# A fill order that also asks for free PSUM banks: the two attentions of an encoder trunk on one Trainium2 core

## The chip, the core and the metric

The kernel runs on one NeuronCore of a Trainium2 chip. The metric is the device time of one launch in microseconds (us), median of several runs. The engines have one instruction queue each, in order: TensorE (PE in the profile), VectorE (DVE), ScalarE (ACT), GpSimd (POOL) and SyncE (SP), which issues nearly all DMAs.

## The reference, cut to what matters

512 tokens of width 1024 go through two layers, all in fp32. Layer A is differential attention with rotary positions, layer B chunked attention with a relative bias over keys and values that are projected once; each is followed by a SwiGLU FFN, and a LayerNorm closes every part.

```python
# layer A, for each of 8 heads and each block i of 128 queries (kend = 128 * (i + 1))
sc = einsum('bqhmd,bkhmd->bhmqk', q[:, q0:kend], k[:, :kend])      # m: two maps
p = softmax(where(allowed, sc, neg)); a = p[:, :, 0] - lam * p[:, :, 1]
outs.append(einsum('bhqk,bkhe->bqhe', a, v[:, :kend]))
...
o = rms_norm(concatenate(outs), subln_g) * (1.0 - lambda_init)     # then @ w_o
# layer B, for each of 16 heads
p = softmax(q @ k_band + bias); o = p @ v_band                     # then @ w_o
# behind each: x = layer_norm(alpha * x + mix); x = layer_norm(alpha * x + swiglu(x))
```

## The kernel before

Every fp32 operand of a large product is split into a high and a low part that TensorE takes at its fast rate, so a projection step is three matmuls (high by high, high by low, low by high) of 512 or 256 columns. All instructions of all engines are written in the order in which the Python program runs; nothing reorders them later. That order comes from a model in the program: `Modelled` and `Model` keep, for each block of a tile, when it is written (`there`) and when it is last used (`used`), by fixed costs per engine, and `clk[0]` is the modelled time of TensorE. `later` and `chain` put the work of the other engines into a list with a modelled time; it is issued when `clk[0]` has come that far.

**Attention A** (lines 1053 to 1136, `unit_a` and `attention_a`) has 32 units, 8 heads by 4 query blocks. A unit has four steps on TensorE: `s`, the scores `sc`, in one bank for each of the two maps; `at`, the transposes of the mixed probabilities `e`; `o`, the product with the values; `ot`, the transpose of the normalised result `sq`. Between `s` and `at` stands the chain for `e`: on DVE a masked pass over each bank of scores with a row maximum (`CUSTOM_DVE_ANT_0`), on ACT two exponentials, on DVE a reciprocal, a factor `c` and the mix. Between `at` and `o` ACT copies `aT`; between `o` and `ot` ACT squares, POOL takes a power and DVE scales (`sq`). `STEPS` says which unit each step takes in an iteration: s(i), o(i-2), ot(i-3), at(i-1). **Attention B** (`unit_b`, `values_b`, `attention_b`) has 8 pairs of heads by 4 query blocks; its steps are `s` (`sc_b`), `at` (transposes `pt_b`) and, once for each pair, `v` (`po`).

Between these steps stand **fills**: matmuls of the projections of later heads (`q_ps`, `k_ps`, `va_ps`; in layer B `bq_ps`, `bk_ps`, `vb_ps`) and, when these are through, of the first part of the output projection (`oa`, `ob`). `weave` takes both streams. A number from the attention is a wish for so many ns of fill, kept as a credit. A function from it is a wait: fill is issued until the function says yes, and what was issued counts as credit, so that less follows. The waits of before ask by `there` whether what a step reads is written in the model.

PSUM has eight banks here: the pool `psp` holds two for each of the names `pj` (projections), `sm`, `sc0` and `sc1`. In attention A a unit's scores take both banks of `sc0`, `at` and `ot` take those of `sm` in turn, `o` those of `sc1`. In attention B the scores take `sc0`, and `pt_b` and `po` take one of `sm` and one of `sc1`. A matmul that opens a bank waits on the chip until the last reader of what stood there is through; in the model that only moves `clk[0]` (`model.unused` in `passed`).

Of the kernel before, what the change touches and what calls it, by code (L numbers as in the profile page):

```python
# [19 lines left out]
P = 128  # L20
# [8 lines left out]
HALF = 512  # L29
# [104 lines left out]
def trunk(ctx, tc, x, a_w_qkv, a_lambda, a_subln_g, a_w_o, kv_w, b_w_q, b_rel_bias, b_w_o,  # L134
          ln_g, ln_b, ffn_w_in, ffn_w_out, cos_t, sin_t, out):
    nc = tc.nc
    model = Model()
# [13 lines left out]
    psp = ctx.enter_context(tc.tile_pool(name="psp", bufs=2, space=PS))  # L151
# [3 lines left out]
    clk = [0.0]  # L155
    popped = [0.0]
    serial = itertools.count()
    pending = []
    slots = {}

    def name_of(a):
        return a.tensor.name
# [27 lines left out]
    def there(*tiles, late=0.0):  # L190

        names = [name_of(t) for t in tiles]
        return not any(n in p_[3] for p_ in pending for n in names) and all(
            model.ready(t) + late <= clk[0] for t in tiles)

    def mm(out_, lhsT, rhs, start, stop, cost=1.0):
        settle([name_of(lhsT), name_of(rhs)])
        nc.tensor.matmul(out_, lhsT, rhs, start=start, stop=stop)  # L198
        passed(out_, (lhsT, rhs), cost * (out_.free_size() / 2.4 + 13), start)
# [34 lines left out]
    def tick(everything=False):  # L234
        while pending and (everything or min(pending)[0] <= clk[0]):
            run_first()
# [580 lines left out]
    values_done = [0]  # L817
# [118 lines left out]
    qk = {}  # L936
# [88 lines left out]
    vt = []  # L1025
# [81 lines left out]
    def attention_a():  # L1107
        units = [(h, qt) for h in range(HA) for qt in range(NT)]
        live = {}
        nu = len(units)  # L1110
        for i in range(nu + max(step[1] for step in STEPS if step[0] != "fill")):
            rates = FA[0] if i < FA[2] else FA[1] if i < nu else FA[3]
            for kind, n in STEPS:
                if kind == "fill":
                    yield rates[n]
                    continue
                if not 0 <= i - n < nu:
                    continue
                h, qt = units[i - n]
                if kind == "s":  # L1120
                    yield lambda: h in qk
                    yield lambda: there(*qk[h])
                    live[i] = [unit_a(h, qt), None]
                    done["n"] = i + 1
                elif kind == "o":
                    yield lambda: 2 * values_done[0] > h and there(live[i - n][1], vt[0][:, h * P:(h + 1) * P])
                else:
                    yield lambda: there(live[i - n][1])
                if kind == "at":
                    done["s"] = i - n == nu - 1  # L1130
                live[i - n][1] = next(live[i - n][0])
                if kind == "ot":
                    del live[i - n]
                    done["o"] = h - (qt < NT - 1)
        tick(True)
# [31 lines left out]
    x1d = [dram.tile([S, D], F32, name=f"x1d_{l}") for l in range(2)]  # L1167

    weave(attention_a(), fill(FILL_A, qk_a, "va", o_proj(oTh, oTl, lambda t: x[0, t * P:(t + 1) * P, :], 0, "oa")))
    tick(True)  # L1170
    phase.close()
# [59 lines left out]
    qk = {}  # L1231
# [7 lines left out]
    vt = []  # L1239
# [12 lines left out]
    held = {}  # L1252
# [33 lines left out]
    biases = {}  # L1286
# [66 lines left out]
    def attention_b():  # L1353
        units = [(p, qt) for p in range(HB // 2) for qt in range(NT)]
        live = {}
        nu = len(units)
        load_bias(0)
        for i in range(nu + max(step[1] for step in STEPS_B if step[0] != "fill")):
            rates = FB[0] if i < FB[2] else FB[1] if i < nu else FB[3]
            for kind, n in STEPS_B:  # L1360
                if kind == "fill":
                    yield rates[n]
                    continue
                if not 0 <= i - n < nu:
                    continue
                p, qt = units[i - n]
                if kind == "s":
                    yield lambda: p in qk
                    yield lambda: there(*qk[p], *biases[p])
                    live[i] = [unit_b(p, qt), None]  # L1370
                    live[i][1] = next(live[i][0])
                    done["n"] = i + 1
                elif kind == "at":
                    yield lambda: there(live[i - n][1])
                    done["s"] = i - n == nu - 1
                    next(live.pop(i - n)[0])
                elif kind == "v" and qt == NT - 1:
                    yield lambda: there(*held[p][1], *held[p][2])
                    values_b(p)
                    done["o"] = p  # L1380
                    yield FBV
                elif kind == "prep":
                    if qt == 1:
                        prepare_b(p)
                    if qt == PREP_B:
                        yield lambda: 2 * values_done[0] > p
                        split_values(p)
                    if qt == NT - 1 and p + 1 < HB // 2:
                        load_bias(p + 1)
        tick(True)  # L1390
# [50 lines left out]
```

## Time and profile before

| | |
|---|---|
| median of 3 runs | 1220.28 us (1219.87 to 1220.51) |
| the profiled execution | 1220.33 us, its span 1218.6 us |
| PE busy | 1186.4 us (97% of the span) |
| DVE busy | 880.6 us (72%) |
| ACT, POOL busy | 554.7 us (46%), 428.2 us (35%) |
| mean granted TensorE clock | 0.994 of full speed |

The span runs from the first to the last instruction of the profiled execution; its time has 1.7 us more around that. Attention A with its fills lies from 47 us to about 223 us, the first FFN and what leads to layer B up to 610 us, attention B up to about 830 us, and the second FFN is the rest. PE rows at line 198 are `mm`, at line 203 transposes; most rows of the other engines are at line 76, where the model issues them, so they are told apart by their tiles. A PE row's length has the pipeline in it: the rate is read from the starts of rows that follow each other.

### The profile page before, as it was taken

The page shows a single profiled execution, that of the slowest core. Times are in us where ns is not written, and L with a number is a line of the kernel's source. Part 1 is how long each engine was busy: PE and PEld are TensorE (multiplying, and loading weights), DVE is VectorE, ACT ScalarE, POOL GpSimd, SP SyncE. Part 2 cuts the span into 40 slices and gives each one's busy share as a digit, 9 for nine tenths or more (in the row PEclk, how much of TensorE's full clock was granted, in tenths as well). Part 3 has the DMA queues.
Part 4 walks back from the last instruction along what each step waited for, and adds up shares of the span by engine and source line. Part 5 has one row for each costly group of instructions (what it writes and reads, how often), then busy time and mean ns, then how long its engine had stood idle before and what let it go on. Part 6 is the DMA issues. An engine that isn't in the chain of part 4 may idle for free.

```text
span 1218.6 us, 20002 instructions
## 1 busy us (share of the span) xinstructions
PE 1186.4 (97%) x7640; PEld 1076.5 (88%) x7640; DVE 880.6 (72%) x1451; ACT 554.7 (46%) x1049; POOL 428.2 (35%) x410
## 2 busy tenths in 40 slices
PE   7999999999999999999999999989999999999997
PEld 7878888789999999888897998968999999998886
DVE  3688797489999998431745677674899999983327
ACT  3467666344444444332236676662454444433220
POOL 1126253414666663001223242213236665510022
PEclk9999999999999999999999999999999999999999
DMA  8444232443555444423244243315433333352321
GB/s 262 127 105 121 75 102 85 162 139 103 149 146 148 143 122 150 136 96 128 97 131 132 75 122 95 105 52 190 122 104 104 105 104 105 105 196 98 104 70 69
DMA packets 164192, 145.75 MB, mean 120 GB/s; under 512 B 6096, under 2 KB 137456, under 8 KB 164096
## 3 DMA queue, kind: packets, MB, share of 16 engines
q1 hardware_dynamic: 164096, 144.47, 39.5%
q8 instruction: 60, 0.98, 0.3%
q14 instruction: 36, 0.29, 0.1%
HBM read 127.63 MB, written 13.67 MB: 116 GB/s over the span
## 4 chain that ended last, share of the span: by engine, by line
PE 90%; DVE 6%; ACT 2%; issue 1%; POOL 1%; DMA 0%; DVEq 0%; SPq 0%; ACTq 0%; POOLq 0%
PE m L198 31%; PE gu L198 6%; PE c L198 5%; PE a L198 5%; PE b L198 5%; PE d L198 4%; PE vb_ps L198 4%; PE bk_ps L198 3%; PE bq_ps L198 3%; PE va_ps L198 3%; PE k_ps L198 3%; PE q_ps L198 3%; PE ob L198 2%; PE oa L198 2%; PE sc_b L198 2%; PE po L198 1%
## 5 line engine op out<-in xcount | busy, mean ns | idle before, releaser
L76 POOL TENSOR_TENSOR sums<-raw_u 128x512 f32<-128x512 f32 x38 | 48.9, 1288 | 167.7 <-DVE s3lo L76 148.7
L76 POOL TENSOR_TENSOR lo_fo<-raw_fo,hi_fo 128x1024 fp32r<-128x1024 f32 x8 | 19.1, 2389 | 215.8 <-ACT hi_fo L76 215.8
L76 ACT ACTIVATE sg<-sg 128x512 f32<-128x512 f32 x38 | 24.0, 632 | 137.8 <-DVE sg L76 137.8
L76 POOL TENSOR_TENSOR sums<-raw_g,sums 128x512 f32<-128x512 f32 x38 | 75.4, 1984 | 0.0
L76 POOL TENSOR_TENSOR sums<-raw_g,raw_u 128x512 f32<-128x512 f32 x38 | 68.7, 1808 | 0.0
L76 DVE TENSOR_TENSOR alo<-raw_g,ahi 128x1024 fp32r<-128x1024 f32 x38 | 67.4, 1773 | 0.1
L76 ACT CAST s3hi<-sums 128x1024 fp32r<-128x1024 f32 x38 | 40.0, 1052 | 59.6 <-POOL sums L76 59.6
L76 ACT CAST hi_fk<-raw_fk 128x1024 fp32r<-128x1024 f32 x28 | 29.5, 1052 | 74.6 <-PE d L198 71.1
L76 DVE TENSOR_TENSOR lo_fk<-raw_fk,hi_fk 128x1024 fp32r<-128x1024 f32 x28 | 33.9, 1221 | 26.9 <-ACT hi_fk L76 26.9
L76 POOL TENSOR_TENSOR sums<-sums,raw_g 128x512 f32<-128x512 f32 x38 | 51.6, 1357 | 3.9 <-DMA raw_g<-in_ffn_w_in_dram 1.1
L76 DVE TENSOR_TENSOR s1lo<-sums,s1hi 128x1024 fp32r<-128x1024 f32 x38 | 48.3, 1271 | 0.0
L76 DVE TENSOR_TENSOR ulo<-raw_u,uhi 128x512 fp32r<-128x512 f32 x38 | 46.7, 1228 | 0.0
L76 ACT CAST hi_fo<-raw_fo 128x1024 fp32r<-128x1024 f32 x16 | 16.9, 1054 | 64.5 <-PE d L198 64.5
L76 DVE TENSOR_TENSOR s3lo<-sums,s3hi 128x1024 fp32r<-128x1024 f32 x38 | 46.1, 1214 | 0.1
L76 POOL TENSOR_TENSOR rs<-rs,mexp 128x1 f32<-128x1 f32 x16 | 15.8, 987 | 79.4 <-DVE rs L76 79.4
L76 DVE TENSOR_TENSOR m<-m,m 128x256 f32<-128x256 f32 x76 | 31.6, 416 | 15.9 <-PE m L198 15.9
L198 PE MATMUL m<-T1h,s1hi 128*128 128x256 f32 x152 | 43.0, 283 | 0.0
L198 PE MATMUL m<-T1l,s1hi 128*128 128x256 f32 x152 | 43.0, 283 | 0.0
L198 PE MATMUL m<-T1h,s1lo 128*128 128x256 f32 x152 | 43.0, 283 | 0.0
L198 PE MATMUL m<-T2g,s1hi 128*128 128x256 f32 x152 | 43.0, 283 | 0.0
L198 PE MATMUL m<-T2b,s1hi 128*128 128x256 f32 x152 | 43.0, 283 | 0.0
L198 PE MATMUL m<-T2g,s1lo 128*128 128x256 f32 x152 | 43.0, 283 | 0.0
(612 smaller groups left out, 4814.0 us busy)
## 6 DMA issues: line engine op xcount, KB each, us to landing
raw_g<-in_ffn_w_in_dram SPq DMA_DIRECT2D x44, 512.0 KB, 4.0
raw_u<-in_ffn_w_in_dram SPq DMA_DIRECT2D x44, 512.0 KB, 5.2
raw_fk<-in_ffn_w_out_dram SPq DMA_DIRECT2D x28, 512.0 KB, 3.7
raw_fo<-in_ffn_w_out_dram SPq DMA_DIRECT2D x16, 512.0 KB, 3.7
skew<-extd SPq DMA_DIRECT2D x16, 320.0 KB, 6.1
raw_va<-in_a_w_qkv_dram SPq DMA_DIRECT2D x8, 512.0 KB, 4.9
raw_q<-in_a_w_qkv_dram SPq DMA_DIRECT2D x8, 512.0 KB, 5.0
raw_k<-in_a_w_qkv_dram SPq DMA_DIRECT2D x8, 512.0 KB, 4.5
```

The costliest lines, as they stand in the source:

```text
L76: return issue(*args, **kwargs)
L198: nc.tensor.matmul(out_, lhsT, rhs, start=start, stop=stop)
```

## The change

A new function `clear` asks of the model whether the banks that the next step will open are out of use: of each name it takes as many of the oldest banks as the step needs, and wants that no deferred instruction names them and that their last modelled use is not after `clk[0]`. Every wait ahead of a step on TensorE in both attentions now asks for that too, so that fills are issued until then. No instruction is added or removed.

```diff
+    def clear(*tags):
+
+        names = [n for tag in dict.fromkeys(tags) for n in slots[(psp.name, tag)][-2:][:tags.count(tag)]]
+        return not any(n in p_[3] for p_ in pending for n in names) and all(
+            model.used.get((n, i), 0.0) <= clk[0] for n in names for i in range(HALF // P))
...
-                    yield lambda: there(*qk[h])
+                    yield lambda: there(*qk[h]) and clear("sc0", "sc0")
...
-                    yield lambda: 2 * values_done[0] > h and there(live[i - n][1], vt[0][:, h * P:(h + 1) * P])
+                    yield lambda: 2 * values_done[0] > h and there(live[i - n][1], vt[0][:, h * P:(h + 1) * P]) and clear("sc1")
                 else:
-                    yield lambda: there(live[i - n][1])
+                    yield lambda: there(live[i - n][1]) and clear("sm")
...
-                    yield lambda: there(*qk[p], *biases[p])
+                    yield lambda: there(*qk[p], *biases[p]) and clear("sc0", "sc0")
...
-                    yield lambda: there(live[i - n][1])
+                    yield lambda: there(live[i - n][1]) and clear("sm", "sc1")
...
-                    yield lambda: there(*held[p][1], *held[p][2])
+                    yield lambda: there(*held[p][1], *held[p][2]) and clear("sm", "sc1")
```

The order on TensorE differs in three stretches, which in the trace of before lie at 77.9 to 136.6 us and 164 to 223 us (attention A) and at 722 to 776 us (attention B); on the other engines instructions move by a few places inside the same stretches. In the changed kernel line 198 has become 204 and line 203 has become 209. In the rows below the first number behind a name is the query block of the unit (for `sc` and `pt_b` the map or head follows), and the last one only tells buffers apart.

**First stretch, TensorE, from the transposes of the first head's query block 3 (77.91 us in the trace) on.** Before:

```order
L203 MATMUL at_3_889<-ident,e_3_733 128x128 x4
L198 MATMUL sc_1_0_921<-ks_779,qs_715 128x256
...
L198 MATMUL o_3_931<-va_323,aT_3_897 128x128
...
L203 MATMUL ot_2_941<-ident,sq_2_883 128x128
L198 MATMUL q_ps_849<-xTh_a,hi_q_708 128x512
...
L203 MATMUL at_0_962<-ident,e_0_873 128x128
L198 MATMUL sc_2_0_973<-ks_779,qs_715 128x384
...
L198 MATMUL o_0_983<-va_323,aT_0_964 128x128
L198 MATMUL q_ps_849<-xTh_a,hi_q_708 128x512
...
L203 MATMUL ot_3_1016<-ident,sq_3_938 128x128
```

And with the change:

```order
L209 MATMUL at_3_889<-ident,e_3_733 128x128 x4
L204 MATMUL q_ps_849<-xTh_a,hi_q_708 128x512
...
L204 MATMUL sc_1_0_958<-ks_779,qs_715 128x256
...
L209 MATMUL ot_2_979<-ident,sq_2_883 128x128
L209 MATMUL at_0_986<-ident,e_0_873 128x128
L204 MATMUL k_ps_938<-xTh_a,hi_k_804 128x512
...
L204 MATMUL sc_2_0_1018<-ks_779,qs_715 128x384
...
L204 MATMUL o_0_1028<-va_323,aT_0_989 128x128
L209 MATMUL ot_3_1045<-ident,sq_3_976 128x128
L209 MATMUL at_1_1052<-ident,e_1_965 128x128 x2
L204 MATMUL sc_3_0_1065<-ks_779,qs_715 128x512
```

Between `at_3` and `sc_1` stand now 24 fills where there were none, between `ot_2` and `at_0` none where there were 9, and between `at_0` and `sc_2` 12 where there were none. From `sc_2` to `at_2` no fill is left; before, 21 fills stood between `at_0` and `at_2`.

**Second stretch, VectorE, the sixth head's query blocks 2 and 3 (184 us in the trace).** Before:

```order
L76 ISA e_3_2181,nm_3_2182<-sc_3_1_2176,mask 128x512
...
L76 TENSOR_TENSOR krc_2208<-kr_2201,cosb 128x512
L76 TENSOR_TENSOR lo_oa_0_2213<-raw_oa_0_1726,hi_oa_0_2211 128x1024
L76 TENSOR_TENSOR lo_oa_1_2216<-raw_oa_1_1846,hi_oa_1_2214 128x1024
L76 TENSOR_TENSOR oTl<-ot_0_2196,oTh 128x128
L76 RECIPROCAL r_3_2184<-s_3_2183 128x2
...
L76 SCALAR_TENSOR_TENSOR e_3_2181<-e_3_2181,c_3_2263 128x512
```

And with the change:

```order
L76 ISA e_2_2126,nm_2_2127<-sc_2_1_2121,mask 128x384
...
L76 TENSOR_TENSOR krc_2168<-kr_2161,cosb 128x512
L76 TENSOR_TENSOR lo_oa_0_2173<-raw_oa_0_1726,hi_oa_0_2171 128x1024
L76 TENSOR_TENSOR lo_oa_1_2176<-raw_oa_1_1846,hi_oa_1_2174 128x1024
...
L76 SCALAR_TENSOR_TENSOR e_2_2126<-e_2_2126,c_2_2248 128x384
L76 ISA e_3_2261,nm_3_2262<-sc_3_0_2251,mask 128x512
...
L76 SCALAR_TENSOR_TENSOR e_3_2261<-e_3_2261,c_3_2347 128x512
```

The two low parts `lo_oa` stood between the masked pass and the mix of query block 3; they now stand between those of query block 2. Between `sc_2` and `at_2` of that block 90 fills are written on PE.

**End of attention A, TensorE, from the last head's first scores (204.99 us in the trace).** Before:

```order
L203 MATMUL at_2_2547<-ident,e_2_2428 128x128 x3
L198 MATMUL sc_0_0_2552<-ks_2321,qs_2170 128x256
...
L198 MATMUL o_2_2570<-va_323,aT_2_2551 128x128
...
L203 MATMUL ot_1_2577<-ident,sq_1_2512 128x128
...
L203 MATMUL at_3_2592<-ident,e_3_2495 128x128 x4
L198 MATMUL sc_1_0_2598<-ks_2321,qs_2170 128x256
```

And with the change:

```order
L209 MATMUL at_2_2541<-ident,e_2_2465 128x128 x3
...
L204 MATMUL sc_0_0_2559<-ks_2254,qs_2255 128x256
...
L204 MATMUL o_2_2569<-va_323,aT_2_2546 128x128
...
L209 MATMUL ot_1_2578<-ident,sq_1_2529 128x128
L209 MATMUL at_3_2581<-ident,e_3_2517 128x128 x4
L204 MATMUL sc_1_0_2600<-ks_2254,qs_2255 128x256
```

Before, three fills stood behind `sc_0` and three behind `ot_1`, the last ahead of the units that run out without any. Now three stand ahead of `sc_0`, none follows, and all other fills have moved further forward. In attention B the moves are smaller: at 723 us, 24 fills of 256 columns that stood behind `sc_b_3` now stand as 36 ahead of `pt_b_1`, and later groups move by three to six matmuls.

## Rows read from the trace of the kernel before

**Rows 1.** The page's chain that ended last, by engine:

```profile
PE 90%; DVE 6%; ACT 2%; issue 1%; POOL 1%; DMA 0%; DVEq 0%; SPq 0%; ACTq 0%; POOLq 0%
```

**Rows 2.** Windows: us, busy by engine, granted PE clock, DMA share, GB/s:

```profile
76.60:136.60 60.00, 57.10 (x353) 49.70 (x353) 49.77 (x135) 41.22 (x121) 27.35 (x43) 1.00 0.39 105
...
164.00:209.00 45.00, 43.31 (x279) 38.22 (x277) 37.10 (x99) 29.25 (x86) 18.90 (x32) 1.00 0.33 95
209.00:223.00 14.00, 10.26 (x55) 8.36 (x56) 8.08 (x30) 7.50 (x28) 4.23 (x12) 0.88 0.01 3
...
722.00:776.00 54.00, 53.96 (x304) 46.61 (x303) 40.53 (x111) 37.45 (x98) 15.71 (x29) 1.00 0.33 98
```

**Rows 3.** PE's waits, whole span: waited for: us in total, times, longest:

```profile
PE pt_b L203 <- DVE e_b L76: 5.3, 3, 2.8
PE at L203 <- DVE e L76: 3.8, 3, 1.5
...
PE at L203 <- DVE oTl L76: 1.0, 1, 1.0
```

**Rows 4.** PE timeline, first stretch: start, length, line, operation [idle before, releaser]:

```profile
77.91 0.60 PE L203 MATMUL at<-ident,e 128*128 128x128 f32 x4
...
80.26 0.48 PE L198 MATMUL q_ps<-xTh_a,hi_q 128*128 128x512 f32 x1
...
84.06 0.30 PE L203 MATMUL at<-ident,e 128*128 128x128 f32 x1 [1.45 <-DVE e L76]
...
92.02 0.49 PE L203 MATMUL at<-ident,e 128*128 128x128 f32 x3
```

**Rows 5.** DVE timeline: masked pass and mix of 384 keys, at 87 and 212 us:

```profile
87.26 0.55 DVE L76 CUSTOM_DVE_ANT_0 e<-sc,mask 128x384 f32<-128x384 f32 x1
...
90.86 0.62 DVE L76 SCALAR_TENSOR_TENSOR e<-e,c 128x384 f32<-128x384 f32 x1
...
211.55 0.55 DVE L76 CUSTOM_DVE_ANT_0 e<-sc,mask 128x384 f32<-128x384 f32 x1
...
214.34 0.62 DVE L76 SCALAR_TENSOR_TENSOR e<-e,c 128x384 f32<-128x384 f32 x1
```

**Rows 6.** PE timeline, two waits later in the first stretch:

```profile
105.10 0.33 PE L203 MATMUL ot<-ident,sq 128*128 128x128 f32 x1 [0.31 <-DVE sq L76]
...
120.28 0.66 PE L203 MATMUL at<-ident,e 128*128 128x128 f32 x4 [1.04 <-DVE oTl L76]
```

**Rows 7.** PE timeline, the listed waits of the second stretch up to 209 us:

```profile
165.18 0.39 PE L198 MATMUL sc<-ks,qs 128*128 128x256 f32 x1 [0.18 <-DVE nm L76]
...
168.54 0.33 PE L203 MATMUL ot<-ident,sq 128*128 128x128 f32 x1 [0.33 <-DVE sq L76]
...
188.38 0.66 PE L203 MATMUL at<-ident,e 128*128 128x128 f32 x4 [0.86 <-DVE e L76]
```

**Rows 8.** DVE timeline ahead of the wait at 188.38 us:

```profile
184.01 2.35 DVE L76 TENSOR_TENSOR lo_oa<-raw_oa,hi_oa 128x1024 fp32r<-128x1024 f32 x2
...
187.57 0.75 DVE L76 SCALAR_TENSOR_TENSOR e<-e,c 128x512 f32<-128x512 f32 x1
```

**Rows 9.** DVE and POOL timelines: one form on DVE alone and beside POOL:

```profile
97.83 0.68 DVE L76 TENSOR_TENSOR krc<-kr,cosb 128x512 f32<-128x512 f32 x1
...
162.04 2.88 DVE L76 TENSOR_TENSOR krc<-kr,cosb 128x512 f32<-128x512 f32 x1
...
161.76 2.61 POOL L76 TENSOR_TENSOR lo_va<-raw_va,hi_va 128x1024 fp32r<-128x1024 f32 x1 [2.49 <-ACT hi_va L76]
```

**Rows 10.** PE timeline, fills behind the end of attention A, early and later:

```profile
220.81 0.63 PE L198 MATMUL oa<-hi_oa,oTl 128*128 128x512 f32 x1
221.23 0.63 PE L198 MATMUL oa<-hi_oa,oTh 128*128 128x512 f32 x1
...
223.46 0.39 PE L198 MATMUL oa<-lo_oa,oTh 128*128 128x512 f32 x1
223.69 0.39 PE L198 MATMUL oa<-hi_oa,oTl 128*128 128x512 f32 x1
```

## The prediction, made before the changed kernel had run

> **What bounds the kernel now.** I read the chain that ended last first: nine tenths of it is PE's own work [rows 1]. The change adds and removes no instruction, so PE's work stays what it is, and only the time in which PE has nothing to do inside the two attentions can go or come. The order of the two programs says where: three stretches, 77.9 to 136.6 us, 164 to 223 us and 722 to 776 us. The windows give what lies idle there, span less PE's busy time [rows 2]: 60.00 - 57.10 = 2.9 us, 45.00 - 43.31 = 1.7 us up to 209 us, 14.00 - 10.26 = 3.7 us at the end of attention A, and 0.04 us in attention B. The list of PE's waits then says what kind they are [rows 3]. Nearly all are waits for data: `at` for the mixed `e`, 3.8 us in three waits, `pt_b` for `e_b`, 5.3 us in three. The waits of `pt_b` cannot go: the third moved stretch has 0.04 us idle, so they lie where the order stays. Waits for a PSUM bank, which the change asks about, are few inside the moved stretches: 1.04 us for `oTl`, the last reader of a bank of `sm` [rows 6], and 0.18 us for `nm`, whose masked pass frees `sc0` [rows 7]. So the direct effect is at most 1.2 us in 1220. What matters more is that, by asking, the program deals out the same fills differently, and data waits go or come with that.
>
> **The change, term by term.** A fill of 512 columns costs 0.23 us, from two starts that follow each other [rows 10].
>
> *Term 1, 77.9 to 92 us.* Before, PE waits 1.45 us for `e` at 84.06 us [rows 4]. Now 24 fills stand ahead of `sc_1`. From 77.91 to 80.26 us PE issued `at_3`, `sc_1`, `o_3` and `ot_2` with small unlisted waits, 2.35 us; I count 1.9 us without these. So `at_0` comes at 77.9 + 1.9 + 24 x 0.23 = 85.3 us, later than 84.06 us, when its `e` was there: that wait goes. Then come 12 fills, 2.8 us, and `sc_2` at 88.3 us with what `at_0` takes. From there to `at_2` no fill is left. Before, that way from `at_0` on took 92.02 - 84.06 = 7.96 us [rows 4] with 21 fills (4.8 us), so PE's own steps there are about 3.1 us. But `at_2` needs the `e` of `sc_2`, and from the first masked pass to the end of the mix took 90.86 + 0.62 - 87.26 = 4.2 us there, and 214.34 + 0.62 - 211.55 = 3.4 us at the end of the attention [rows 5]. With 0.9 us for the scores and the step between engines ahead of it, `at_2` starts at 88.3 + 0.9 + 4.2 = 93.4 us, and 2.2 us of that are a new wait, on DVE and ACT. By then PE has issued 36 fills where it had issued 30; before, `at_2` at 92.02 us plus six fills, 1.4 us, is 93.4 us too. **Term 1 is 0.** With the shorter chain it is -0.8 us; with the chain held up once behind POOL (rival 2) +2.2 us.
>
> *Term 2, 92 to 136.6 us.* Listed waits of 0.31 and 1.04 us [rows 6], together 1.35 us. The second is the one real bank wait, and the new order issues 15 and 27 fills behind `at_0` and `at_3` around there. In exchange the low parts of the next weights now stand between a masked pass and a mix on DVE, so some of it comes back. **Term 2 is -0.9 us**, between -1.35 and +0.5 us, the last if a new wait as long as the listed longest, 1.5 us [rows 3], comes with neither gone in full.
>
> *Term 3, 164 to 209 us.* The wait of 0.86 us at 188.38 us [rows 7] is for an `e` that was late because two `lo_oa`, 2.35 us on DVE, were issued between its masked pass and its mix [rows 8]. They now stand a query block earlier, where 90 fills are between scores and transposes. It goes. The bank wait of 0.18 us at 165.18 us goes too, but behind it PE meets `ot` at 168.54 us, which waited 0.33 us for a `sq` [rows 7] that DVE finishes no earlier than before: the `krc` ahead of it is the one that took 2.88 us [rows 9]. So that one comes back longer. **Term 3 is -0.9 us**, between -1.4 us (all three listed waits) and 0.
>
> *Term 4, 209 to 223 us.* There the fills have run out, and PE is paced by the chain for `e`. Now they run out one step earlier: the last head's `sc_0` has no fill behind it. Nine fills, 2.1 us, and PE's own steps stand between the scores of the block before and their `at_3`, against a chain of 4.2 us or a little more for 512 keys. What a missing cover costs I estimate at **+0.4 us**, between 0 and the longest wait for `e`, 1.5 us [rows 3].
>
> *Term 5, attention B.* 0.04 us idle [rows 2], so nothing to gain: **0**, between -0.3 us (small waits that PE's busy time may hide) and +0.8 us if a `pt_b` meets its `e_b` too early. PE's end of attention B, with the long waits for `e_b`, is written in the same order as before.
>
> On the other queues the moves change no sum of work. On SP two groups of DMAs (the copies for `ks` and the shifted `qsw`) change places; both feed a head that begins several units later, so the fills of the units between hide them, and without that cover a `s` step would wait for `ks`.
>
> Sum: 0 - 0.9 - 0.9 + 0.4 + 0 = -1.4 us. The profiled execution took 1220.33 us, which is the median of the runs, 1220.28 us, within 0.1 us. So **1218.9 us**. About 0.2%, 2.4 us, is what a measurement of this kernel can tell from no change, so I forecast the same.
>
> **Rivals.** *Rival 1, clearly faster.* The fills land where the waits were and nothing comes back: all of the 2.9 and 1.7 us idle in the first two stretches goes [rows 2], -4.6 us, 1215.7 us; from -2.4 us on it counts as faster. For it: the waits are short and many, and almost any fill ahead of them covers them. Against it: the run from `sc_2` to `at_2` without a fill, which by DVE's rows must wait.
>
> *Rival 2, slower.* DVE's chain for `e` in that same run is held up behind POOL. A `krc` that takes 0.68 us alone took 2.88 us while POOL was in a `lo_va` of 2.61 us [rows 9], 2.2 us more. DVE's queue is in order, so the masked passes and the mix behind it come later, and now no fill covers them; PE waits. One such meeting between 88 and 93 us makes the sum -1.4 + 2.2 = +0.8 us, which is still the same; from two on it is +3.0 us, 1223.3 us. For it: in the new order POOL's `lo_va` and both rotary products stand closer to these units. Against: POOL is busy less than half of that window, 27.35 of 60 us [rows 2]. The Trainium skill, SBUF — State Buffer, "Who interferes with whom", says that VectorE and GpSimd share a port pair, taken as an exclusive lock for a whole instruction. By that rule every DVE instruction with two SBUF inputs that meets a POOL read is stretched so; the 2.88 us agrees with it.
>
> *Rival 3, nothing.* The bank waits were too small, and what one place gains the next returns: 1220.3 us, inside the same class.
>
> A clock loss rides on term 4 only: the granted clock is 0.88 at the end of attention A and 1.00 in the other three stretches [rows 2], and behind its waits fills start 0.42 us apart instead of 0.23 us [rows 10], that is at 1.2 instead of 2.4 GHz. A longer wait there would prolong it; the bound of term 4 holds a part.
>
> **How the numbers follow.** The forecast, a sum within 2.4 us of nothing on the faster side: 0.48. Rival 3: 0.12. Rival 1: 0.30. Rival 2: 0.10. Same is 0.48 + 0.12 = 0.60, faster 0.30, slower 0.10. For the range I go from the forecast down to the middle of rival 1 and up over one meeting on POOL with term 4 at its bound: the low end is 1215.8 us, and the high end 1220.33 + 0.8 + 1.1 = 1222.2 us; beyond these I leave about one in ten on each side.
>
> **What would show it.** Right: no wait of `at` at the place of 84.06 us, a new one of about 2 us for `e` at the `at_2` some 9 us later; the waits for `oTl` at 120 us and for `e` at 188 us gone; idle from 209 to 223 us a little larger; attention B unchanged within 0.5 us. Wrong: if the `at_2` without fills finds its `e` ready, rival 1 holds; if rows of DVE beyond 2 us stand in the chains of these units, rival 2; and if the idle of the whole attention moves by over 3 us, a term is missing.

## The result and the profile after

The changed kernel took **1229.36 us** (median of four runs, 1228.69 to 1229.80) where before took 1220.07 us beside it: a ratio of 1.0079, with a 95% interval of 1.0065 to 1.0092. It is slower by 9.3 us, where 1218.9 us and "the same" were forecast. A second measurement of the unaltered change (e5 below) gave 1.0065 (1.0052 to 1.0077).

The page's chain that ended last shows the share of each engine; beside [rows 1] nothing stands out, since 9 us are 0.7% of the span:

```profile
PE 90%; DVE 5%; ACT 2%; DMA 1%; issue 1%; POOL 0%; SPq 0%; DVEq 0%; ACTq 0%; POOLq 0%
```

Where the time went is read from landmarks. These are five rows of PE of the changed kernel (start, length, line, operation):

```profile
79.59 0.60 PE L209 MATMUL at<-ident,e 128*128 128x128 f32 x4
141.41 0.49 PE L209 MATMUL at<-ident,e 128*128 128x128 f32 x3
163.07 0.49 PE L209 MATMUL at<-ident,e 128*128 128x128 f32 x3
256.82 1.04 PE L209 MATMUL xt_ps<-ident,oa_x 128*128 128x128 f32 x8
1219.45 0.39 PE L204 MATMUL d<-hi_fo,hs_10l 128*128 128x512 f32 x1
```

The same five steps before are 77.91 us [rows 4] and these four:

```profile
136.57 0.49 PE L203 MATMUL at<-ident,e 128*128 128x128 f32 x3
158.22 0.49 PE L203 MATMUL at<-ident,e 128*128 128x128 f32 x3
246.54 1.03 PE L203 MATMUL xt_ps<-ident,oa_x 128*128 128x128 f32 x8
1210.50 0.39 PE L198 MATMUL d<-hi_fo,hs_10l 128*128 128x512 f32 x1
```

The differences are 1.68, 4.84, 4.85, 10.28 and 8.95 us. So 1.68 us were lost before any instruction had moved (each execution's own: in the other profiles the same row comes 1.6 us earlier to 1.6 us later than before); **3.16 us in the first moved stretch; 0.01 us where the order is unchanged; 5.43 us in the second stretch with the end of attention A**; and 1.33 us came back later: 0.4 us in attention B's moved stretch and 1.1 us at the end of attention B, whose order is unchanged, less 0.2 us lost between. Together 8.95 us, which is 1229.28 less 1220.33 us. Below, "stretch 1" and "end A" mean the first and the second of these two intervals.

The windows of the changed kernel (us, busy by engine, granted clock, DMA share, GB/s), to be read beside [rows 2]:

```profile
76.60:136.60 60.00, 55.20 (x337) 48.67 (x336) 49.13 (x124) 39.04 (x113) 25.14 (x41) 0.97 0.38 100
...
209.00:223.00 14.00, 11.18 (x60) 9.00 (x59) 9.42 (x38) 8.08 (x31) 4.07 (x13) 0.88 0.13 38
223.00:236.00 13.00, 9.98 (x45) 8.10 (x45) 5.01 (x16) 5.51 (x18) 3.49 (x9) 0.74 0.01 3
```

In the first stretch PE is now idle for 4.8 us instead of 2.9 us, and its clock fell to 0.97. The end of attention A has become longer and slower: it reaches to 233 us, and at a mean of 0.74 about half of its last 13 us ran at 1.2 instead of 2.4 GHz.

The waits of the first stretch hang on two rows. This is DVE's timeline and POOL's, then PE's:

```profile
97.00 3.63 DVE L76 SCALAR_TENSOR_TENSOR qs<-qrc,qs 64x512 fp32r<-64x512 f32 x2
```

```profile
97.69 2.39 POOL L76 TENSOR_TENSOR lo_va<-raw_va,hi_va 128x1024 fp32r<-128x1024 f32 x1
```

```profile
94.81 0.55 PE L209 MATMUL at<-ident,e 128*128 128x128 f32 x3 [0.59 <-DVE e L76]
...
101.36 0.30 PE L209 MATMUL ot<-ident,sq 128*128 128x128 f32 x1 [1.37 <-DVE r L76]
102.38 0.66 PE L209 MATMUL at<-ident,e 128*128 128x128 f32 x4 [0.72 <-DVE e L76]
...
103.60 0.63 PE L204 MATMUL q_ps<-xTh_a,hi_q 128*128 128x512 f32 x1
104.02 0.63 PE L204 MATMUL q_ps<-xTl_a,hi_q 128*128 128x512 f32 x1
...
124.18 0.30 PE L209 MATMUL ot<-ident,sq 128*128 128x128 f32 x1 [1.48 <-DVE r L76]
```

The scaled queries `qs` met POOL's `lo_va` and took 3.63 us; the `sq` and the mix behind them in DVE's queue came late, PE waited 1.37 and 0.72 us, and then its products started 0.42 us apart. At 124.18 us it is the same, without half clock, with a `qs` of 2.51 us beside POOL's `ksw`.

The meeting itself is not new. Before, the same `lo_va` ran from 98.52 us for 2.38 us and held a factor `c` of 128x1, which takes 0.22 us elsewhere:

```profile
99.05 1.86 DVE L76 SCALAR_TENSOR_TENSOR c<-s,r,nlam 128x1 f32<-128x1 f32 x1
```

The `at` behind it started at 102.90 us without a listed wait, because nine fills stood ahead of it. With the change no fill stands between the `o` at 99.16 us and the two waits: what the new order took away is the cover.

### The profile page after: what moved, and what is told of

It reads as the page before. It is cut to its first block, busy times and chain, and to the rows that moved or that the text cites. A ratio compares the mean times of both kernels' runs of the same rounds, so it can differ in the third digit from the quotient of the medians.

```text
span 1227.5 us, 20008 instructions
## 1 busy us (share of the span) xinstructions
PE 1190.4 (97%) x7640; PEld 1080.1 (88%) x7640; DVE 882.5 (72%) x1451; ACT 554.7 (45%) x1049; POOL 425.7 (35%) x410
## 4 chain that ended last, share of the span: by engine, by line
PE 90%; DVE 5%; ACT 2%; DMA 1%; issue 1%; POOL 0%; SPq 0%; DVEq 0%; ACTq 0%; POOLq 0%
PE m L204 31%; PE gu L204 6%; PE c L204 5%; PE a L204 5%; PE b L204 5%; PE d L204 4%; PE vb_ps L204 4%; PE va_ps L204 4%; PE bk_ps L204 3%; PE bq_ps L204 3%; PE q_ps L204 3%; PE k_ps L204 2%; PE ob L204 2%; PE oa L204 2%; PE pt_b L209 2%; PE sc_b L204 1%
## 5 line engine op out<-in xcount | busy, mean ns | idle before, releaser
L204 PE MATMUL m<-T3h,s3hi 128*128 128x256 f32 x152 | 43.0, 283 | 0.0
```

## The experiments

All ratios are to before on the same chip. "End A" and "stretch 1" of a profile are the differences to the profile of before over the two intervals above.

### The change in parts: e1, e2, e3

```diff
-  there(*qk[h]) and clear("sc0", "sc0")
+  there(*qk[h]) and (i >= 17 or clear("sc0", "sc0"))   # e1; e2: i < 17
```

and likewise at `o` and `at`/`ot`; in e3 the questions of attention A are taken out.

> The question about banks is asked only for the first 17 of the 32 units of attention A; from there on, and in attention B, the order is that of before. Theory P (POOL): the loss of the first moved stretch is DVE work held up behind POOL (the scaled queries qs of 3.63 us at 97 us, of 2.51 us at 121 us) with no fill left to cover it, then some steps at half clock; it is 3.1 us, so about 3 us slower than before, and a qs of over 3 us stands again near 97 us. Theory F (fills): nearly all of the loss comes from the end of attention A, where the fills have run out earlier; this kernel is then within 1 us of before. Theory S (start): the 1.7 us that the changed kernel is late before its first moved instruction belong to that execution alone; here the first transposes of attention A come within 0.5 us of before. If they are tied to the program, they come 1.7 us late here too.

> The question is asked only from unit 17 of attention A on; the first stretch and attention B are ordered as before. Theory F: the end of attention A is what costs; some 5 us slower than before, 4 us of it between 209 us and the end of the output projection, with half clock behind the waits. Theory P: the loss lies in the first stretch and in DVE rows held up behind POOL; then this kernel is less than 2 us slower. My prediction had -0.5 us for this part.

> The question is asked only in attention B. The traces of before and of the change differ by -1 us over attention B. All theories: between -1.5 and 0 us against before. If it is slower by 1 us or more, the gain in attention B of the one changed execution was that execution's own.

| kernel | median us | ratio (95%) | stretch 1 | end A | clock 204 to 234 us |
|---|---|---|---|---|---|
| e1, early units | 1222.04 | 1.0008 (1.0000 to 1.0017) | +1.60 | -1.01 | 1.00 |
| e2, late units | 1227.75 | 1.0051 (1.0037 to 1.0065) | 0.00 | +3.33 | 0.89 |
| e3, attention B | 1219.35 | 0.9988 (0.9979 to 0.9997) | +1.10 | -1.17 | 1.00 |
| e5, whole change again | 1228.16 | 1.0065 (1.0052 to 1.0077) | +3.15 | +4.37 | 0.89 |

Most of the loss comes with the late units. Attention B alone gains 1.5 us by the medians (0.4 to 2.6 us); in the profiles its moved stretch is 0.4 us shorter in all six kernels that ask there. The early part kept its long `qs` (3.63 us) and both waits (1.35 and 0.72 us), but not the half clock, and cost 1.6 us in stretch 1 rather than 3.2 us; by the medians it cost about 1 us, where theory P had about 3.

Executions in which stretch 1 is unaltered differ there by 0 or by 1.0 to 1.1 us, as in e3. That is a POOL meeting too. These are the mix and POOL's `ksw` in before, then in e3, whose orders are the same there:

```profile
100.95 0.35 DVE L76 SCALAR_TENSOR_TENSOR e<-e,c 128x128 f32<-128x128 f32 x1
...
101.08 1.39 POOL L76 TENSOR_TENSOR ksw<-ksw,sinb 128x512 f32<-128x512 f32 x1 [0.18 <-DMA ksw<-kr]
```

```profile
100.79 1.45 DVE L76 SCALAR_TENSOR_TENSOR e<-e,c 128x128 f32<-128x128 f32 x1
...
100.81 1.29 POOL L76 TENSOR_TENSOR ksw<-ksw,sinb 128x512 f32<-128x512 f32 x1
```

In the seven unaltered profiles that lose 1.0 us, `ksw` starts with the mix or up to 0.1 us ahead of it, and the mix takes 1.35 to 1.45 us; in the others `ksw` starts about 0.1 us or more behind it, and the mix takes 0.35 us. So whether POOL waits some 0.2 us for a DMA or not is worth 1 us here. Whether part of e1's 1.60 us is of this kind is not shown.

> The changed kernel once more, unaltered. The three parts alone came to +0.7, +6.2 and -1.5 us by their medians, together +5.4 us, while the whole change came to +9.3 us in its first runs. If the parts add up, it is 4 to 7 us slower than before; if the whole is more than its parts, 8 to 10 us slower. In its first profile q_ps rows stood 0.42 us apart at 103.6 us behind two waits, and 2 us went there; the early part alone had the same waits and no such rows. If that belongs to single executions, the clock in that place is 1.00 in this profile, or the times of this kernel spread by about 2 us.

The parts add up to 0.8 - 1.2 + 5.1 = 4.7 per mille (3.7 with the second measurement of the late part, e15 below), the whole to 6.5 and 7.9. In both profiles of the whole the half clock stands in stretch 1 (granted 0.91 from 92 to 110 us, 1.00 in e1), which is 1.6 us of the gap. Where the rest of it lies stays open.

### The meeting with POOL: e4

```diff
-  e.tensor_sub(lo, raw, hi)          # e: POOL for the third value chunk
+  # same place in the order, issued on DVE for keys va_2_0 and va_2_1
```

> The changed kernel in its own order on every engine, but the two low parts of the third value chunk (lo_va, 1024 columns each, about 2.4 us on POOL) are issued on DVE instead, at the place in DVE's order where POOL's would have been issued. Theory P: the qs near 97 us takes 1.4 us instead of 3.63 us, the waits of 1.5 and 0.9 us for ot and at at 101 and 102 us and the half clock behind them go, and the kernel is about 2 to 3 us faster than the changed one, less what two more rows of about 1.2 us on DVE cost. Theory F: nothing changes in the time (within 0.7 us of the changed kernel), since the late chain is late for want of fills.

It took 1224.92 us, 1.0035 (1.0023 to 1.0048): 3.0 to 4.4 per mille less than the two measurements of the whole. Of its rows on DVE, `qs` and the low part that POOL no longer does, and what is left of the two waits of PE:

```profile
96.28 1.40 DVE L77 SCALAR_TENSOR_TENSOR qs<-qrc,qs 64x512 fp32r<-64x512 f32 x2
...
98.18 1.21 DVE L77 TENSOR_TENSOR lo_va<-raw_va,hi_va 128x1024 fp32r<-128x1024 f32 x1
```

```profile
100.56 0.66 PE L210 MATMUL at<-ident,e 128*128 128x128 f32 x4 [1.15 <-DVE e L77]
```

The 2.2 us of the meeting are gone although DVE has 2.4 us more to do, and one wait of 1.15 us stands where two of 1.37 and 0.72 us stood. The second meeting, with `ksw`, stayed, and so did a wait of 1.55 us behind it. Stretch 1 costs 0.54 us instead of 3.15, and the clock there is 1.00. Against e1, which had the meeting and a clock of 1.00 too, the gain is 1.1 us; that the half clock, the other 1.6 us, went with the meeting is not shown by one profile. The profile thus accounts for 2.6 us of the 3.7 to 5.4 us that e4 gains by the medians, and where the rest lies is not shown. The mechanism of the prediction's rival 2 is shown: a row of POOL stretches one of DVE, and PE waits for what stands behind. The Trainium skill, SBUF — State Buffer, "Who interferes with whom", gives the rule for it (a port pair that VectorE and GpSimd share, held for a whole instruction); these rows agree: the line counts two `qs`, of 0.7 us each when alone, and the second ended half a microsecond after POOL's row did.

### What the end of attention A lacks: e6, e7, e8, e12, e17

> The question is asked for units 17 to 25 alone, not for the last six: most products of stretch 2 stay moved as in the late part alone, but nine output products (oa) instead of none are left behind the last head's first scores, where before has six. Theory F (the end runs without a reserve): the 6.2 us of the late part are gone, the kernel is within 1.5 us of before, and the clock from 209 to 228 us is 0.9 or more. Theory M (the moved order of stretch 2 itself costs, wherever the last fills stand): 3 to 6 us slower than before.

> The order of before, but the six output products (oa, 1.4 us) that stand behind the last head's first scores are issued ahead of at_2 of head 6 instead, some 3 us earlier; the question about banks is nowhere asked. Theory F: this alone brings the loss of the late part: 3 to 6 us slower than before, clock below 0.9 between 209 and 228 us. Theory M: the place of six products is worth no more than the products themselves, at most 1.4 us slower.

> The late part alone, with 18 products of 512 columns more whose result is overwritten, put where PE waits at the end of attention A: 6 ahead of the transposes of at_3 of head 6, 2 ahead of its o_3, 4 ahead of o_0 and 6 ahead of at_3 of head 7, each into the bank that the waiting instruction writes. They last 18 x 0.23 = 4.1 us, in waits that add up to 4.7 us there. Theory C (part of the loss is TensorE at 1.2 GHz behind the waits): the granted clock from 209 to 228 us rises from 0.82 to near 1.00, oa and sc rows stand at their short distance, and 2 to 3 us come back against the late part alone, so 3 to 4 us slower than before. If the clock costs nothing on the path (theory F with its chain alone), no time comes back, or up to 1 us is lost.

```diff
-  there(live[i - n][1]) and clear("sm")
+  there(live[i - n][1]) and (not 17 <= i < 26 or clear("sm"))   # e6, alike at all three
-  yield rates[n]
+  yield rates[n] + (1386.0 if i == 27 and n == 1 else 0.0)      # e8, in before
+  busy(pt, "at", h, qt)    # e7: products into the bank that the next row writes
```

| kernel | median us | ratio (95%) | end A | listed waits 204 to 234 us | clock there |
|---|---|---|---|---|---|
| e6, question off for the last six units of attention A | 1222.73 | 1.0018 (1.0009 to 1.0027) | +2.24 | 3.8 | 0.94 |
| e7, late part, waits filled | 1222.28 | 1.0014 (1.0005 to 1.0024) | +3.21 | 2.3 | 0.94 |
| e8, before, six products spent early | 1219.90 | 0.9995 (0.9986 to 1.0004) | -1.07 | 3.9 | 1.00 |
| e12, before, nine products of cover | 1219.96 | 0.9994 (0.9985 to 1.0003) | -1.18 | 3.9 | 1.00 |
| e17, before, blocks close together | 1220.20 | 0.9999 (0.9988 to 1.0010) | -1.37 | 3.8 | 1.00 |

Without the question in the last six units 1.8 per mille of the 4.1 to 5.1 are left (e6). So more than half of the loss arises there; what the units 17 to 25 lose was not traced, and the 2.2 us lie between the ranges of both theories. But the six products that the late part no longer has behind the last scores are worth nothing (e8): **theory F falls**. Filling the waits with products whose result nobody reads brought 2.7 to 3.7 per mille back against the late part (e7), more than the 2 to 3 us that theory C expected, although they cover nothing and the clock was still 0.94; its one profile shows only 0.1 to 1.1 us of that in end A, so where the rest of it comes from is not shown.

The next theory was the cover between the last scores of head 6 and their transposes, which falls from 24 products to nine:

> The order of before with no question anywhere, but of the 24 output products that stand between the last scores of head 6 (sc_3, 512 keys) and the transposes of their weights (at_3), 15 are issued ahead of sc_3 instead, so that nine are left, as in the late part of the change; behind the last head's first scores the six of before remain among these nine. Theory L (what the late part costs is the cover between these scores and their at_3, and the clock that falls behind the wait there): a wait of 1 to 1.6 us for e stands at this at_3, granted clock under 0.9 from 209 to 228 us, and the kernel is 3 to 6 us slower than before. If the loss needs more of the change than that (the fills moved around the values in stretch 2), it is within 1.5 us of before.

```diff
-  yield rates[n]
+  yield rates[n] + {(26, 2): 2980.0, (27, 1): -2350.0, (27, 2): -630.0}.get((i, n), 0.0)
```

It fell too: with nine products the `at_3` at 209.14 us waited for nothing. And it is not that small products of several blocks come close together:

> The order of before, no question anywhere, but of head 6 the 24 output products that e12 issues between o_0, ot_3 and at_1 are issued ahead of o_0 instead, so that o_0, ot_3, at_1, sc_3, o_1, ot_0, at_2 follow each other with six products among them, as in the late part. Cover behind sc_3 as in e12 (12 products to at_3). Theory Bunch (small products of several blocks that come close together make the in-order queues of DVE, ACT and POOL serve one block behind the other, and the chain for e comes out longer): a wait of over 1 us at at_3 or at_2 of head 6 and 2 to 6 us slower than before. Rival: within 1 us of before.

```diff
+  {(26, 0): 5960.0, (26, 1): -2350.0, (26, 2): -630.0, (27, 1): -2350.0, (27, 2): -630.0}
```

What does differ is how PE spent the same 30 us. Windows of before, the change, e12 and the late part (e15, below), in that order:

```profile
204.00:234.00 30.00, 26.05 (x138) 21.52 (x137) 12.13 (x45) 14.10 (x44) 13.28 (x22) 0.94 0.20 65
```

```profile
204.00:234.00 30.00, 24.16 (x120) 19.68 (x119) 17.21 (x62) 16.10 (x59) 8.56 (x23) 0.83 0.07 19
```

```profile
204.00:234.00 30.00, 26.04 (x146) 21.51 (x145) 13.51 (x50) 16.40 (x52) 14.76 (x24) 1.00 0.21 67
```

```profile
204.00:234.00 30.00, 23.16 (x120) 18.75 (x119) 14.39 (x55) 15.04 (x50) 10.82 (x23) 0.89 0.06 19
```

PE is idle for 4 us in before and e12 and for 6 to 7 us in the other two, which also run slower, at 0.83 and 0.89. (The one profile of before has 0.94 itself. In e1, e3, e8, e12 and e17 the clock is 1.00, and their end A is 1.0 to 1.4 us shorter than before's; against them the late part loses that much more than the tables say.) PE's waits in that window, of the late part and then of e12 (us in total, times, longest):

```profile
PE at L209 <- DVE e L76: 4.1, 3, 1.6
PE o L204 <- ACT aT L76: 2.0, 3, 1.0
PE at L209 <- DVE oTl L76: 0.7, 1, 0.7
```

```profile
PE at L203 <- DVE e L76: 1.6, 1, 1.6
PE ot L203 <- DVE sq L76: 1.1, 2, 1.0
PE o L198 <- ACT aT L76: 0.9, 2, 0.6
PE at L203 <- DVE oTl L76: 0.3, 1, 0.3
```

Three waits for `e` instead of one, 6.8 us in all instead of 3.9. The rest is read from the last head's `at_3` to the last `ot`, in e15 and then in e12:

```profile
222.15 1.12 PE L209 MATMUL at<-ident,e 128*128 128x128 f32 x4 [1.61 <-DVE e L76]
...
230.98 0.27 PE L209 MATMUL ot<-ident,sq 128*128 128x128 f32 x1
```

```profile
220.17 0.66 PE L203 MATMUL at<-ident,e 128*128 128x128 f32 x4 [1.61 <-DVE e L76]
...
226.48 0.27 PE L203 MATMUL ot<-ident,sq 128*128 128x128 f32 x1
```

Both issue the same 34 rows there and list no wait inside; e15 takes 8.83 us and e12 6.31 us. These 2.5 us are the half clock.

### The queues of DVE and ACT: e13 to e16, e18

At equal cover the chain for `e` of head 6's block 3 is longer in the late part. DVE's masked pass starts there 2.6 us after PE began the last product of its first bank of scores (at 202.50 us in e15; in e12 it is 0.4 us, after 203.87 us). The pass in e15 and in e12:

```profile
205.11 0.68 DVE L76 CUSTOM_DVE_ANT_0 e<-sc,mask 128x512 f32<-128x512 f32 x1
```

```profile
204.30 0.69 DVE L76 CUSTOM_DVE_ANT_0 e<-sc,mask 128x512 f32<-128x512 f32 x1 [1.23 <-PE sc L198]
```

In e15 it stands behind an `sq` that waits 0.98 us for POOL; ACT's exponentials then stand behind the copy `aT` of the block before. Four runs move rows in those two queues alone, and e15 is the late part unaltered; PE's order is the same in all five.

> The late part alone once more, unaltered, to compare on the same chip: 4.5 to 8 us slower than before. Its runs spread from 1224.6 to 1228.2 us, and the profiled one was the fastest of them; if the spread is the clock at the end of attention A, this profile shows more rows at the long distance there when its time is longer.

> The late part alone, and of it one DVE instruction moved: the sq of head 6's block 0 (the product that waits 0.98 us for POOL's rr at 204.58 us) is issued behind the masked pass of block 3 instead of ahead of the mix of block 2. Every other instruction on every engine keeps its place. Theory Q (DVE's order: the masked pass stands behind a row that waits for another engine): the masked pass starts about 1 us earlier, the wait for e at at_3 falls from 1.4 to about 0.5 us, and with it part of the half clock behind goes: 1 to 3 us faster than the late part. Rival (the e chain is late at other places too, and a gain here is given back at the next wait): within 0.7 us of the late part.

> The late part alone, but on DVE the masked pass of head 6's block 3 stands ahead of that sq, of the mix of block 2 and of one oTl, which follow it unaltered. Theory Q: the masked pass starts within 0.3 us of its scores, 1.6 us earlier; at_2 may wait 0.5 us for the mix that is now later, at_3 waits less than 0.3 us; 1 to 3.5 us faster than the late part. Rival: as before, within 0.7 us of the late part, or slower if at_2's wait replaces at_3's.

> The late part alone, and in it for head 6's block 3 two moves: on DVE its masked pass ahead of the sq of block 0, the mix of block 2 and one oTl (as in the run before), and on ACT its exponentials ahead of the copy aT of block 2, which waits for the transposes of that block. Theory Q2 (two queues in a row hold the chain, and moving one alone leaves it held by the other): e of block 3 is ready 1 to 1.4 us earlier, the wait at at_3 falls from 1.4 to under 0.5 us, and 1 to 4 us come back against the late part (4.1 to 5.1 per mille slower than before). Rival (what is gained at at_3 comes back at the next waits, since the end is paced by the same chain block after block): the wait at at_3 goes, but the time is within 0.7 us of the late part.

> The late part alone, and on ACT the exponentials of four blocks (head 6 block 3, head 7 blocks 0, 1 and 2) are issued right behind their scores, ahead of the square (sq), the cast (oTh) and the copy (aT) of the blocks before; nothing else moves on any engine. Theory Q3 (ACT's order over the whole end holds the chain): the listed waits from 204 to 234 us fall from 6.8 us in the late part towards the 3.9 us of e12, the clock there rises to 0.94 or more, and 2 to 5 us come back against the late part: 0 to 3 us slower than before. Rival (no single queue holds it; each move hands the wait on): within 1 us of the late part, 4 to 6 us slower than before.

```diff
 DVE  lo_oa_3
+DVE  masked pass e_3 (both halves)      e14, e16
 DVE  sq_0                               e13: behind the masked pass
 DVE  r_2, c_2, mix e_2, oTl
-DVE  masked pass e_3 (both halves)
 ACT  sq_1, oTh
+ACT  exponentials e_3                   e16; e18: four blocks, ahead of sq, oTh and aT
 ACT  aT_2
-ACT  exponentials e_3
```

| kernel | median us | ratio (95%) | end A | clock 204 to 234 us |
|---|---|---|---|---|
| e15, late part again | 1225.78 | 1.0041 (1.0028 to 1.0054) | +4.28 | 0.89 |
| e13, `sq` moved | 1225.72 | 1.0048 (1.0033 to 1.0062) | +5.30 | 0.89 |
| e14, masked pass moved | 1226.39 | 1.0042 (1.0026 to 1.0058) | +4.07 | 0.89 |
| e16, masked pass and exponentials | 1225.55 | 1.0037 (1.0022 to 1.0051) | +3.63 | 0.89 |
| e18, exponentials of four blocks | 1229.64 | 1.0079 (1.0065 to 1.0093) | +8.28 | 0.72 |

None helps. In e13 and e14 the wait at `at_3` stayed at 1.41 and 1.43 us. In e16, where ACT's rows moved too, it did go, and two others took most of its place. PE's rows of e15 (`at_3` and `o_3`), and of e16 (`at_2`, which waits for nothing in e15, then the same two):

```profile
209.17 0.63 PE L209 MATMUL at<-ident,e 128*128 128x128 f32 x4 [1.42 <-DVE e L76]
...
210.67 1.16 PE L204 MATMUL o<-va,aT 128*128 128x128 f32 x8 [0.40 <-ACT aT L76]
```

```profile
206.30 0.55 PE L224 MATMUL at<-ident,e 128*128 128x128 f32 x3 [0.44 <-DVE oTl L92]
...
208.96 0.63 PE L224 MATMUL at<-ident,e 128*128 128x128 f32 x4
...
210.94 1.16 PE L219 MATMUL o<-va,aT 128*128 128x128 f32 x8 [0.87 <-ACT aT L76]
```

The wait is handed on, as that run's rival had it. e18 is the telling miss, outside the ranges of both its theories: its listed waits are 6.2 us, no more than the 6.8 us of e15, but the clock is 0.72, and the end takes 4.0 us longer. Which order of the small rows makes the late part's waits was **not settled**; that no single queue holds them was.

### Both costs away, and a version against both: e9, e10, e11

> The changed kernel in its whole order with both suspected costs taken away: the two low parts of the third value chunk on DVE, as alone before (ratio 1.0035 there against 1.0065 and 1.0079 of the whole change), and overwritten products ahead of the waits at the end of attention A: 6 before at_3 of head 6, 2 before its o_3, 4 before o_0, 4 before at_2 and 6 before at_3 of head 7. If POOL's hold on DVE in stretch 1 and the waits with their half clock at the end of attention A are what the change costs, the two savings add up: -1 to +2 us against before. If a cost is missing from the account, it stays 3 us or more slower.

1222.04 us, 1.0014 (1.0005 to 1.0023), as expected: of the 6.5 to 7.9 per mille, 5 to 6.5 go with the POOL meeting and the filled waits together. Its clock from 204 to 234 us is 1.00, stretch 1 costs 0.55 us and end A 1.74 us.

> A version meant to beat both: the question is asked in attention B alone (-1.5 us by its own run), and at the end of attention A, in the order of before, overwritten products fill the waits: 1 before o_3 and 5 before ot_3 of head 6, 1 before o_0, 2 before o_2 and 6 before at_3 of head 7. The clock stays at 1.00 from 209 to 228 us in every execution, where it was 0.91 in the profile of before and 1.00 in others of the same order. The two add up: 2 to 3 us faster than before. If filling the waits delays the chain, as the transposes come behind the products, it is no faster than the run with attention B alone.

> Before with the same overwritten products at the end of attention A and no question about banks. Theory C: the clock is lost there in part of the executions of before, and 1.4 us with it; 0.3 to 1.2 us faster than before. If the products delay the chain, 0 to 1 us slower.

e10 took 1219.50 us, 0.9990 (0.9981 to 0.9999), and e11 1220.47 us, 1.0000 (0.9991 to 1.0009). Filled waits gain nothing in the order of before: in e1 and e3, which end in that order, the clock is 1.00 there anyway, though the one profile of before has 0.94. The best version by its median is e3, the question in attention B alone: 1.5 us faster than before, with an interval that ends just under 1, of which the rows of the moved stretch show 0.4 us.

## Why the prediction was wrong, step by step

- **Term 1** (0): right in kind. The wait at the place of 84.06 us is gone and the unfilled run ends in a wait of `at_2` for `e`, 0.59 us where 2.2 were expected (with 0.64 us for `nm` ahead of it). At `at_2` the difference had grown from 1.68 to 2.79 us, which is the six fills more (1.4 us) less 0.3 us.
- **Term 2** (-0.9, at most +0.5): **failed.** It was +3.4 us: from 2.79 us at `at_2` to 4.84 us at the end is 2.05 us, and the six fills should have come back, another 1.4 us. The listed waits of [rows 6] did go; the waits of 1.37, 0.72 and 1.48 us for DVE came. The step set their bound at one wait of 1.5 us without looking at what stands on POOL behind the new places of `qs`. That was put under rival 2, with the right size (2.2 us; measured 3.63 - 1.40 = 2.23) but at 88 to 93 us; it came at 97 and 121 us, and the half clock behind it, 1.6 us, was not in its price: the prediction let the clock ride on term 4 only.
- **Term 3** (-0.9, at most 0): **failed, by little.** The wait of 0.86 us of [rows 7] did go, and the one for `sq` came back longer, as said. But the gain was handed on: the changed kernel waits there for `ks`, `sq`, `aT` and `va`, 0.3 to 0.7 us each and 2.0 us together, where before lists 1.4 us. At head 6's `at_3`, ahead of which both have issued the same products, it had lost 0.6 us in this stretch (the wait of that row left out), the late part in e15 0.0 us. The row before and with the change:

```profile
207.72 0.60 PE L203 MATMUL at<-ident,e 128*128 128x128 f32 x4
```

```profile
214.56 0.63 PE L209 MATMUL at<-ident,e 128*128 128x128 f32 x4 [1.43 <-DVE e L76]
```

- **Term 4** (+0.4, at most 1.5): **failed, and is the largest miss.** It was +4.9 us: the 5.43 us of the second interval less term 3's. The late part alone costs 4.1 to 5.1 per mille, 5 to 6 us. The text counted the nine fills of cover rightly, and `at_3` did wait; but e12 has the same nine and no wait there, so the count alone does not decide it, and the text bounded the whole end by one longest wait. The chain for `e` paces each later block too: three waits for `e` instead of one, 6.8 us of listed waits instead of 3.9. The ends of e15 and e12 differ by 5.5 us, of which 2.9 us are listed waits and 2.5 us the clock, which was said to "ride on term 4": 0.83 to 0.89 in all five profiles of e2, e4, e5, e15 and the change, 0.94 in before, e6 and e7, and 1.00 in e1, e3, e8, e12 and e17. Which rows of DVE, ACT and POOL make the chain late there stays open.
- **Term 5** (0, at best -0.3): close. The moved stretch gained 0.4 us in all six profiles of kernels that ask there, a little more than the bound; the 1.5 us of e3's medians have an interval from 0.4 to 2.6 us.
- **The rivals.** Rival 1 fell. Rival 2 had the sign, one of the two causes and the size of one meeting, but a chance of only 0.10, because it was tied to one window; its signs of being wrong did name it: rows of DVE beyond 2 us in the chains of these units. By itself it would not have made the change slower than the stated range: the early part alone took 1.0008 of before.
- **The range.** Its low end, 1215.8 us, is rival 1 at its full size (1215.7 us) and not at its middle (-3.5 us, 1216.8 us); the miss is at the other end.

## What to carry to other kernels

Where the bound engine is nearly always busy, 97% of the span here, a planner's question that makes it wait less in the model deals out the same filler differently, and the price is set where the filler runs out: cost that stretch as a chain over all its blocks, not as one wait. Price a wait of the matrix engine with the half-speed rows that may follow it, here 1.6 us in the first stretch and 2.5 us at the end of attention A in e15. And before a chain is left without cover, look at what POOL does beside its DVE rows: the meeting was there before too, and cost nothing while fills stood ahead of the next wait.

## What the runs showed of the hardware that was not expected

The same wait is followed by half clock in one execution and not in the next. In attention B, where no order was changed, PE waits 1.22 to 1.24 us for `e_b` in every profile. Rows behind it in e15, then in e2, whose orders are identical:

```profile
659.74 0.90 PE L209 MATMUL pt_b<-ident,e_b 128*128 128x128 f32 x4 [1.24 <-DVE e_b L76]
...
662.72 0.63 PE L204 MATMUL bk_ps<-xTl_b,hi_bk 128*128 128x512 f32 x1
663.14 0.63 PE L204 MATMUL bk_ps<-xTh_b,lo_bk 128*128 128x512 f32 x1
```

```profile
659.94 0.90 PE L209 MATMUL pt_b<-ident,e_b 128*128 128x128 f32 x4 [1.24 <-DVE e_b L76]
...
662.16 0.39 PE L204 MATMUL bk_ps<-xTl_b,hi_bk 128*128 128x512 f32 x1
662.39 0.39 PE L204 MATMUL bk_ps<-xTh_b,lo_bk 128*128 128x512 f32 x1
```

They start 0.42 us apart in the one and 0.23 us in the other, and e15 loses 1.6 us there. It is so in four of the twenty profiles (e5, e13, e15 and e16), all of kernels that ask in the late units of attention A; whether that is more than chance is not shown. So a single profile can show 1 to 2 us at such a place that the next one does not have, and only several of them tell an order's cost from an execution's. The other surprise is that products without any use, put where PE waits, made the late part 3 to 4.5 us faster by its medians.
